# A hybrid decoder layer on one Trainium2 core: the scheduler ranks instructions by the build's timeline model

## The chip, the cores and the metric

The kernel runs on one core of one Trainium2 chip. A core has five engines that run side by side, each through its own queue of instructions in a fixed order: TensorE (PE, matrix products; its weight loads are shown apart as PEld), VectorE (DVE), ScalarE (ACT), GpSimd (POOL) and SyncE (SP). Engines wait for one another by semaphores. An instruction that waits holds up everything behind it in its own queue. DMA transfers are started by instructions of SP, ACT or POOL and then run by themselves.

The metric is the device time of one execution in microseconds (us). The kernel before took 2222.85, 2223.15 and 2224.5 us in three runs; the median is 2223.15 us.

## The reference

One layer of a decoder on 512 tokens of width 2048, in float32, with one batch:

```python
mod = silu(c) @ W_ada + b_ada                # shift1, scale1, gate1, shift2, scale2, gate2
h   = rms_norm(x, norm1_g) * (1 + scale1) + shift1
u   = h @ w_in                               # columns: 3 x 1024 conv, 1024 q, 6 x 256 k/v, 24 gates
y_conv = u_b * causal_conv3(u_c * u_h)       # 1024 channels
y_attn = g0 * compressed + g1 * selected + g2 * sliding_window      # 8 heads of 128, 2 k/v heads
x   = x + gate1 * (concat(rms_norm(y_conv), rms_norm(y_attn)) @ w_out)
h   = rms_norm(x, norm2_g) * (1 + scale2) + shift2
x   = x + gate2 * (relu(h @ w_ff1) ** 2 @ w_ff2)                    # hidden width 8192
return rms_norm(x, normf_g)
```

With 512 tokens there are 8 blocks of 64 tokens and up to 16 may be selected, so the selected branch sees every earlier token, and so does the sliding window of 512. The compressed branch attends to 31 blocks made by a small two-layer network (`compress`).

## The kernel before

**Layout.** Activations lie transposed: 128 channels on the partitions, 512 tokens along the free axis. Weights come as blobs of 128 x 1024 float32 (512 KB).

**Every product is three matmuls.** A float32 operand is split into a high part, rounded to the narrower type that PE takes at full rate, and a low part, the rest. `split`, `weights` (L76) and `hilo` (L799) do this: the high part is a copy on ACT (L83, L89, L800), the low part a subtraction on DVE (L84, L90, L801). `mm3` then issues L93 (high x high), L94 and L95 (the two mixed products). So a weight blob goes through DMA, ACT and DVE before PE can use it: L93 and L94 need only ACT's part of the blob, L95 needs DVE's part; L94 takes the low part of the activations.

**Buffers.** Raw blobs of the first half lie in three `raw` buffers (L72), loaded through SP's queue (L73) and free again when L84 has read them. In the feed-forward part there are six buffers `rw` (L791) for raw blobs, three pairs `hl` (L796) for split ones, two `sg` for sums of blobs and three `gt` for results on their way out.

**Stages, with the stretch of the profiled execution that each takes (us).**

- 0–184: the first projections (`w_kv`, `w_cv`) with the first norm and parts of the modulation vectors `mod`. Its instructions go through `pin` (L67), which calls `tc.keep_in_program_order` while `pinned[0]` is true (set at L98, cleared at L411). Their order is the written one.
- 184–584: the remaining projections (`project`, L429), with `compress` (L446) for the compressed branch, and in turn with them `ada` (L142, its loads at L147, its sums at L134), which works out the rest of `mod` on DVE, one vector of weights after another.
- 584–778: attention (`attention`, L654) over 2 groups of heads and 4 blocks of queries. Scores go to PSUM tiles `s` (three banks, L673–L676), their maxima and exponentials to DVE and ACT; the score's first 32 columns are moved by DVE to `pc` (L683); then come transposes (L719), splits of the transposed probabilities `tt`, and the products with the values in the one bank `pv`. Behind each block follow its squares (L733), their sum over heads (L737) and over channels (L739). Between the blocks `out_conv` (L641) issues the output projection of the conv half: 16 calls with 24 matmuls each into a tile `pw`, and L650 adds the residual.
- 778–794: the norm of the attention half. `tot` (L760) sums the squares; `row_bcast` (L175, L761) takes the root on ACT (L178) behind a table load, makes a diagonal on DVE, spreads it by PE (L197) and copies it on ACT (L182) into `rc`. A loop over eight tiles scales `ya` (L766) and splits it into `mixa` (L769), with the last two calls of `out_conv` at j = 0 and j = 4.
- 794–880: the output projection of the attention half, first 1024 columns (`w_oa`), with the last eight vectors of `mod`; the other 1024 columns (`late_out`) use blobs kept split in spare buffers.
- 880–960: preparation of the feed-forward tokens. `low_tokens` (L888) and `high_tokens` (L897) scale by the second norm and make seven combinations of tokens (B1, U6, T5, B2, T7, B3, T4), each split in high and low. The first products run in between (`ahead`, L962).
- 960–1540: first feed-forward product (`ff1`, L971), 32 steps. Each step loads four blobs, and `operands` (L918) makes seven weight operands of them (sums at L875, splits at L800 and L801); seven products of half size take the place of eight (a Strassen-like scheme). Results are squared, combined, split into `gt` and written to DRAM tensors `g` through POOL's queue (L1015, L1019).
- 1540–1600: the handoff. Token tiles `tk` of the second product are read back from `g` through the same queue (L1121), and the residual from `x1d` (L1086).
- 1600–2140: second feed-forward product, 8 x 4 steps of the same scheme.
- 2140–2222: the last quarter step in plain products (`plain`, L1091) and the final norm (`finish`, L1056).

**What sets the order.** The kernel is written in Tile: the program's text states operations on tiles; a scheduler takes the instructions that the text issues, ranks them by a model of how long each takes, and writes for each engine a queue in the order that the ranking gives. Buffers go to tiles, and waits to instructions, by that order. Only instructions that are kept in program order (the pinned stage) stay as written. So a matmul of `out_conv` needn't stand where the text has it.

## Time and profile before

The rows that the prediction shows aren't repeated here. The span is the time from the first to the last instruction on the core; the profiled execution's own time lies around it.

| what | value |
|---|---|
| median of three runs | 2223.15 us |
| lowest and highest | 2222.85 and 2224.5 us |
| the profiled execution's own time | 2224.19 us |
| its span | 2222.4 us |
| mean granted clock of PE | 0.981 |
| DMA, read and written | 383.00 and 68.16 MB, 203 GB/s |

The busy shares of PE, DVE and the DMA engines in 40 equal slices of the span (55.6 us each, in tenths) and the granted clock:

```profile
PE   6999989999999999799999999999899999999997
DVE  8889978877496687999999999999799999999996
PEclk7999999999999999899999999999999999999998
DMA  8985686954211165276665666658865466366442
```

PE is at least 90% busy in 35 slices of the 40. The lower ones are the first, those that begin at 278, 889 and 1556 us, and the last: the first loads, the projections, the token preparation, the handoff between the two feed-forward products, and the final norm.

How to read the rows below: in a timeline a row has the start, the duration, the engine, the line of the kernel, the operation, output<-inputs with their shapes, and in brackets the idle time of the engine before it with what ended it. In a table of waits a row has the engine, its waiting tile and line, what it waited for, then total us, times and the longest. In a table of groups the numbers are the busy time and the mean ns of one, then the idle time just before the group's instructions. Durations of matmuls overlap, since they are pipelined.

### The profile page before, as it was taken

Reading aid. Unit: us, or ns where it says so; the run is one execution under the profiler, and the core shown is the slowest. Engines: PE = TensorE matmul, PEld = TensorE weight load, DVE = VectorE, ACT = ScalarE, POOL = GpSimd, SP = SyncE. Lnnn points to the kernel's source line nnn. Section 1 sums busy time; section 2 is a strip of 40 time slices with the busy share of each in tenths; the row PEclk is TensorE's granted clock in tenths of the full one; section 3 lists DMA queues with packets and bytes.
Section 4 is the critical chain, followed back from the end, with each engine's and each line's share of the span. In section 5 each row is a group of like instructions: output and inputs, shape, how many; then the busy total and the mean of one; then the engine's idle time right before and its main releaser. Section 6 shows DMA issues by size and latency. Waiting matters only on the chain.

```text
span 2222.4 us, 37637 instructions
## 1 busy us (share of the span) xinstructions
PE 2131.6 (96%) x14942; PEld 1969.9 (89%) x14942; DVE 1918.1 (86%) x2998; ACT 1008.2 (45%) x1468; POOL 193.6 (9%) x366
## 2 busy tenths in 40 slices
PE   6999989999999999799999999999899999999997
PEld 4777778898777779799999999999899999999996
DVE  8889978877496687999999999999799999999996
ACT  4431333222354435665666556666333333333353
POOL 0000000000000001021111111113211011011000
PEclk7999999999999999899999999999999999999998
DMA  8985686954211165276665666658865466366442
GB/s 343 336 323 180 237 313 256 356 216 180 86 39 57 57 266 185 81 233 209 199 196 195 199 211 196 201 190 283 296 241 195 157 237 233 119 237 235 151 146 95
DMA packets 143984, 453.61 MB, mean 204 GB/s; under 512 B 15809, under 2 KB 20161, under 8 KB 143809
## 3 DMA queue, kind: packets, MB, share of 16 engines
q1 hardware_dynamic: 91104, 322.22, 40.4%
q0 software_dynamic: 51616, 127.95, 17.2%
q8 instruction: 117, 1.92, 0.3%
q10 hardware_dynamic: 1088, 1.05, 0.1%
q14 instruction: 59, 0.48, 0.1%
HBM read 383.00 MB, written 68.16 MB: 203 GB/s over the span
## 4 chain that ended last, share of the span: by engine, by line
PE 75%; DVE 13%; ACT 5%; DMA 4%; issue 2%; SPq 0%; DVEq 0%; ACTq 0%; POOL 0%; POOLq 0%
PE pf L95 18%; PE pf L93 18%; PE pf L94 18%; PE ps L94 5%; PE ps L95 5%; PE ps L93 5%; DVE scr L134 3%; DVE wl L84 2%; DMA tk<-g 1%; DVE hl L801 1%; ACT wh L83 1%; PE pw L94 1%; PE pw L95 1%; PE pw L93 1%; PE pt L719 1%
## 5 line engine op out<-in xcount | busy, mean ns | idle before, releaser
L93 PE MATMUL pf<-tk,hl 128*128 128x256 f32 x3576 | 1008.0, 282 | 12.3 <-DMA tk<-g 6.0
L95 PE MATMUL pf<-tk,hl 128*128 128x256 f32 x3576 | 1005.5, 282 | 12.2 <-DVE hl L801 12.2
L94 PE MATMUL pf<-tk,hl 128*128 128x256 f32 x3576 | 1006.7, 282 | 1.3 <-DVE tk L872 1.3
L93 PEld LDWEIGHTS pf<-tk,hl 128*128 128x128 f32 x3576 | 678.2, 190 | 15.3 <-ACT hl L800 8.0
L95 PEld LDWEIGHTS pf<-tk,hl 128*128 128x128 f32 x3576 | 676.7, 190 | 14.8 <-DVE hl L801 14.7
L94 PEld LDWEIGHTS pf<-tk,hl 128*128 128x128 f32 x3576 | 677.0, 189 | 1.7 <-DVE tk L872 1.6
L800 ACT ACTIVATE hl<-rw 128x1024 fp32r<-128x1024 f32 x264 | 278.8, 1056 | 303.6 <-PE pf L95 254.9
L801 DVE TENSOR_TENSOR hl<-rw,hl 128x1024 fp32r<-128x1024 f32 x264 | 321.9, 1219 | 25.6 <-ACT hl L800 25.2
L800 ACT ACTIVATE hl<-sg 128x1024 fp32r<-128x1024 f32 x189 | 200.3, 1061 | 267.7 <-PE pf L95 242.9
L801 DVE TENSOR_TENSOR hl<-sg,hl 128x1024 fp32r<-128x1024 f32 x189 | 230.5, 1221 | 41.7 <-ACT hl L800 41.3
L134 DVE SCALAR_TENSOR_TENSOR scr<-wa,cs 128x1024 bf16<-128x1024 f32 x176 | 211.0, 1220 | 8.1 <-DMA wa<-in_w_ada 8.0
L83 ACT ACTIVATE wh<-raw 128x1024 fp32r<-128x1024 f32 (+1 forms) x105 | 110.8, 1059 | 221.0 <-PE ps L94 105.1
L84 DVE TENSOR_TENSOR wl<-raw,wh 128x1024 fp32r<-128x1024 f32 (+1 forms) x105 | 128.6, 1225 | 56.6 <-ACT wh L83 54.2
L875 DVE TENSOR_TENSOR sg<-sg,rw 128x1024 f32<-128x1024 f32 x126 | 153.5, 1219 | 0.9
L95 PE MATMUL ps<-h_m,wl 128*128 128x512 f32 x360 | 142.8, 397 | 2.5 <-DVE wl L84 2.4
L93 PE MATMUL ps<-h_m,wh 128*128 128x512 f32 x360 | 142.6, 396 | 2.4 <-ACT wh L83 1.2
L94 PE MATMUL ps<-h_m,wh 128*128 128x512 f32 x360 | 141.8, 394 | 0.0
L1049 DVE SCALAR_TENSOR_TENSOR x<-pf,mod,x 128x256 f32<-128x256 f32 x256 | 119.7, 479 | 17.9 <-PE pf L95 14.9
L93 PE MATMUL ps<-h,wh 128*128 128x512 f32 x280 | 113.2, 404 | 13.1 <-ACT wh L83 9.1
L95 PE MATMUL ps<-h,wl 128*128 128x512 f32 x280 | 113.7, 406 | 2.4 <-DVE wl L84 2.4
L94 PE MATMUL ps<-h,wh 128*128 128x512 f32 x280 | 113.3, 405 | 0.0
L1015 POOL DMA_DIRECT2D g<-gt x192 | 101.0, 532 | 86.4 <-DVE gt L872 81.2
(325 smaller groups left out, 2974.1 us busy)
## 6 DMA issues: line engine op xcount, KB each, us to landing
rw<-in_w_f SPq DMA_DIRECT2D x262, 512.0 KB, 4.3
wa<-in_w_ada SPq DMA_DIRECT2D x176, 512.0 KB, 6.2
tk<-g POOLq DMA_DIRECT2D x114, 512.0 KB, 8.1
g<-gt POOLq DMA_DIRECT2D x192, 256.0 KB, 5.0
raw<-in_w_conv SPq DMA_DIRECT2D x32, 512.0 KB, 6.6
raw<-in_w_kv SPq DMA_DIRECT2D x16, 512.0 KB, 5.4
raw<-in_w_cv SPq DMA_DIRECT2D x16, 512.0 KB, 4.5
raw<-in_cmp_w SPq DMA_DIRECT2D x16, 512.0 KB, 5.4
```

What stands on the lines that cost most here:

```text
L83: pin(nc.scalar.activation(wh[:, :cols], raw[:, :cols], AF.Copy))
L84: pin(nc.vector.tensor_tensor(out=wl[:, :cols], in0=raw[:, :cols], in1=wh[:, :cols].bitcast(F32), op=OP.subtract))
L93: pin(nc.tensor.matmul(ps, lh, rh, start=start, stop=False, skip_group_check=more))
L94: pin(nc.tensor.matmul(ps, lh, rl, start=False, stop=False, skip_group_check=more))
L95: pin(nc.tensor.matmul(ps, ll, rh, start=False, stop=stop, skip_group_check=more))
L134: pin(nc.vector.scalar_tensor_tensor(out=scr, in0=w, scalar=1.0, in1=cs[i].rearrange("p a b -> p (a b)"), op0=OP.mult, op1=OP.mult, accum_ ...
L719: nc.tensor.transpose(pt[:, r * P:(r + 1) * P], probs[b, r][:, kb * P:(kb + 1) * P], ident)
L800: nc.scalar.activation(dst[0], src, AF.Copy)
L801: nc.vector.tensor_tensor(out=dst[1], in0=src, in1=dst[0].bitcast(F32), op=OP.subtract)
L875: nc.vector.tensor_tensor(out=dst, in0=x, in1=y, op=op)
L1015: nc.gpsimd.dma_start(out=gd[p // 4][idx[j]][p % 4 // 2][:, p % 2], in_=g[:, j])
L1049: nc.vector.scalar_tensor_tensor(out=xm, in0=src, scalar=gate, in1=xm, op0=OP.mult, op1=OP.add)
```

## The change

One argument of the scheduler's context changes. Without it, instructions are ranked by the scheduler's default model of durations; with it, by a simulated timeline of the build. The text of the kernel, its tiles, pools and buffers stay, and so does `keep_in_program_order` for the first stage.

```diff
@@ -1246,7 +1246,7 @@
     args = {k[3:]: nc.dram_tensor(k, v.shape, mybir.dt.from_np(v.dtype), kind="ExternalInput").ap()
             for k, v in arrays.items()}
     out = nc.dram_tensor("out", OUT_SHAPE, F32, kind="ExternalOutput").ap()
-    with tile.TileContext(nc) as tc:
+    with tile.TileContext(nc, schedule_with_timeline_sim=True) as tc:
         hybrid_layer(tc, args, out)
     r = run_bass_kernel_spmd(nc, [arrays], core_ids=[0])
     return unpack(r.results[0]["out"])
```

What that does to the queues can be listed from the two builds, since each engine's instructions stand in a fixed order:

| engine | instructions | at another place | first difference |
|---|---|---|---|
| PE | 14898 | 5266 | 807th |
| DVE | 2807 | 1617 | 269th |
| ACT | 1409 | 619 | |
| POOL | 363 | 34 | 226th |
| SP | 623 | 78 | 126th |

Each engine's first difference lies behind the pinned stage. The places that the prediction goes through: loads of `raw` stand ahead of some of `ada`'s in SP's queue, and blocks of `compress` alternate with halves of a `project` block on PE; at the start of attention 24 `pw` matmuls stand ahead of the fourth score tile; all `out_conv` matmuls stand ahead of the last block of attention, none behind it; in DVE's queue eight L766 and two L650 stand ahead of the first low split of `mixa`; in the token preparation three L875 sums of weights and the low splits of weights stand ahead of token operations; in the steady steps of the feed-forward products two high products of the next operand stand in front of the 24 matmuls before them; at the handoff the token loads L1121 follow each other in POOL's queue, with the writes L1015 and L1019 behind them.

## Prediction

> **What bounds the kernel now.** I read the page's summary first, then the busy time by stretches (bounds set at the stages), then what TensorE (PE) waited for in each, and single instructions.
>
> ```profile
> span 2222.4 us, 37637 instructions
> PE 2131.6 (96%) x14942; PEld 1969.9 (89%) x14942; DVE 1918.1 (86%) x2998; ACT 1008.2 (45%) x1468; POOL 193.6 (9%) x366
> PE 75%; DVE 13%; ACT 5%; DMA 4%; issue 2%; SPq 0%; DVEq 0%; ACTq 0%; POOL 0%; POOLq 0%
> ```
>
> PE is busy in 96% of the span. No matmul is added or removed, so an order can win only what PE now idles (2222.4 − 2131.6 = 90.8 us) and the share in which its clock is low. Where that lies:
>
> ```profile
> core 0: us, PE busy (x) PEld busy (x) DVE busy (x) ACT busy (x) POOL busy (x), PEclk, DMA share, GB/s
> 0.00:184.00 184.00, 159.57 (x623) 120.21 (x624) 160.30 (x285) 71.76 (x94) 0.20 (x4) 0.94 0.84 313
> 184.00:584.00 400.00, 387.49 (x1937) 323.78 (x1936) 319.41 (x520) 125.44 (x160) 0.00 (x0) 0.99 0.65 243
> 594.00:607.00 13.00, 10.56 (x43) 9.26 (x43) 7.33 (x32) 5.18 (x20) 0.00 (x0) 0.61 0.24 83
> 607.00:778.00 171.00, 165.38 (x859) 130.69 (x858) 128.38 (x313) 82.50 (x216) 0.00 (x0) 1.00 0.14 50
> 778.00:794.00 16.00, 15.68 (x67) 11.84 (x66) 11.86 (x19) 9.41 (x17) 0.00 (x0) 1.00 0.29 99
> 880.00:960.00 80.00, 65.59 (x461) 62.64 (x460) 74.70 (x137) 52.52 (x102) 5.74 (x10) 0.87 0.32 109
> 960.00:1540.00 580.00, 579.50 (x4913) 578.75 (x4912) 534.89 (x715) 359.46 (x507) 112.76 (x215) 1.00 0.64 204
> 1540.00:1600.00 60.00, 51.60 (x414) 50.84 (x414) 46.77 (x63) 24.09 (x32) 18.14 (x34) 0.94 0.99 362
> 1600.00:2140.00 540.00, 540.00 (x4582) 540.00 (x4581) 498.71 (x692) 209.83 (x211) 51.07 (x95) 1.00 0.55 199
> 2140.00:2222.00 82.00, 64.89 (x519) 62.11 (x517) 64.70 (x116) 35.99 (x68) 0.00 (x0) 0.93 0.27 91
> ```
>
> Columns: length, busy time of each engine with its number of instructions, granted clock (1.00 is full), DMA share. The first 184 us hold 24.4 us of the idle time, but their written order stays: nothing to win or lose. The two feed-forward stretches (960–1540 and 1600–2140) idle 0.50 and 0.00 us in 1120: they can only lose. What is open lies between: projections 12.5, start of attention 2.4 and half a clock, attention 5.6, its tail 0.3, token preparation 14.4, the handoff from the first to the second feed-forward product 8.4, the end 17.1; the 5 us left over lie in 794–880, at the first w_oa weights, whose place doesn't change.
>
> **The change part by part.** Every engine keeps its number of instructions; their order changes. In the changed build 5,266 of PE's 14,898 instructions stand at another place, 1,617 of DVE's 2,807, 619 of ACT's 1,409, 34 of POOL's 363 and 78 of SP's 623, the first in each behind the pinned stage. I follow the new order through each stretch.
>
> *Projections and compression, 184–584.*
>
> ```profile
> PE ps L93 <- ACT wh L83: 7.4, 3, 6.1
> SPq L73 <- DVE wl L84: 25.0, 7, 7.4
> ```
>
> First row: PE's largest wait of the stretch (total, times, longest). Second: SP's queue between 240 and 300 us stood 25.0 us for the raw buffers (three, freed by the low split at L84), with weight loads of the modulation vectors (L147) in turn with the raw loads. The new order puts raw loads ahead of some L147 loads and interleaves a compression block with halves of a projection block, so PE has two streams to choose from. A raw load earlier in SP's queue still waits for the same buffer, and now holds the L147 loads behind it, for which DVE's L134 sums wait; those have slack until L650. I take half of the 7.4: −4, between −10 (that and two or three of the small waits) and +4 (the blocked L147 loads cost half of the longest wait, 7.4).
>
> *Start of attention, 594–607.*
>
> ```profile
> 594.28 0.44 PE L93 MATMUL pw<-mix,wh 128*128 128x512 f32 x1
> 597.16 0.50 PE L673 MATMUL s<-kslc,q 128*128 128x160 f32 x1 [2.44 <-DVE pc L683]
> ```
>
> PE stands 2.44 us because the fourth score tile needs a bank that DVE frees at L683. The new order has 24 matmuls of the filler (output projection of the conv half, tile pw) ahead of that fourth score. At 0.25 us each (14.23 us for 57, the tail's first row below) they last 6 us and cover the 2.44. The clock of 0.61 over 13 us costs up to 10.56 × 0.39 = 4.1 more if it follows from the gap. Gain 2.4 to 6.5; I take −5 with −2 and −7 as bounds.
>
> [...]
>
> *Attention, 607–778.*
>
> ```profile
> PE pt L739 <- DVE sr L737: 2.1, 7, 0.5
> PE pv L93 <- ACT tt L89: 1.6, 5, 0.6
> ```
>
> The filler is issued earlier and in larger groups, so more PE work stands between a score and its transposes (8.9 us before, 16.8 after, median, by counting matmuls of each order at their traced spacing). Only 5.6 us are idle; I take half, −3, bounds −5.6 and 0.
>
> *The tail, 778–794: the price.* All filler now stands ahead of the last block, so the norm of the attention half runs bare.
>
> ```profile
> 778.00:794.00 16.00, 14.23 (x57) 10.49 (x57) 1.49 (x2) 1.00 0.29 99
> 778.27 0.60 ACT L733 ACTIVATE sq<-pv 128x512 f32<-128x512 f32 x1 [1.55 <-PE pv L95]
> 780.12 0.35 PE L739 MATMUL pt<-ones,sr 128*128 128x1 f32 x2 [0.24 <-DVE sr L737]
> 780.85 1.06 ACT L83 ACTIVATE wh<-raw 128x1024 fp32r<-128x1024 f32 x1 [1.30 <-PE pw L94]
> 781.93 1.28 ACT L178 ACT_TABLE_LOAD   x1
> 784.60 1.10 PE L197 MATMUL pt<-dg,ones 128*128 128x512 f32 x2
> 785.74 0.60 ACT L182 ACTIVATE rc<-pt 128x512 f32<-128x512 f32 x1 [2.21 <-PE pt L197]
> 788.36 0.68 DVE L90 TENSOR_TENSOR mixa<-ya,mixa 128x512 fp32r<-128x512 f32 x1
> L766 DVE SCALAR_TENSOR_TENSOR ya<-ya,vec,rc 128x512 f32<-128x512 f32 x8 | 5.6, 746 | 1.9 <-ACT rc L182 1.9
> L650 DVE SCALAR_TENSOR_TENSOR x<-pw,mod,raw 128x512 f32<-128x512 f32 x16 | 11.9, 747 | 12.4 <-PE pw L95 12.3
> PE pf L95 <- DVE wl L84: 1.3, 1, 1.3
> ```
>
> First row: of the 16 us, 57 filler matmuls are 14.23; in the changed order there are none. What is left is the chain: square (778.27), sum over partitions, root, the diagonal broadcast (L197), rc, the scaled ya (L766), the split of mixa, the first matmul of w_oa. The root now begins at 783.2, behind a weight split (780.85) and the table load (781.93). That split is gone from ACT's queue here: the table load follows the copies of the square's block and is over when the sum arrives (780.12 + 0.35 and two small DVE steps, about 780.9). So everything from the root on comes 2.3 us earlier: rc at 785.74 − 2.3 = 783.4, done at 784.0. In DVE's new order eight L766 and two L650 stand ahead of the first low split. They follow each other at about 0.66 (the 746 ns of a record overlap): 784.0 + 10 × 0.66 + 0.68 = 791.3. Until then PE can do L197 (1.1), the sum (0.2) and eight high products of the first block (1.9). Idle: 791.3 − 778.3 − 3.2 = 9.8. To that 2 at half a clock (as behind the gap at 594) and 1.5, since the last block has lost its filler as well; minus 1.3, the weight split's wait of the last row, which falls away. Sum +12; bounds +8 (clock stays, last block covered) and +15 (the table load isn't earlier).
>
> *Token preparation, 880–960.* DVE is busy 74.70 of 80: it is the bound.
>
> ```profile
> PE pf L95 <- DVE hl L801: 9.2, 6, 3.1
> 897.46 1.23 DVE L875 TENSOR_TENSOR sg<-rw 128x1024 f32<-128x1024 f32 x1 [1.05 <-DMA rw<-in_w_f]
> ```
>
> The new order puts the low splits of weights (L801) ahead of the token operations, and moves three such L875 sums of 1.22 us out of the stretch into DVE's idle time before 895. At most 3 × 1.22 plus half the 9.2 leave, 8; with rises in the clock (0.87) 12. Against it: the sum at 897.46 waited for a load, and one put ahead of the tokens blocks DVE until it lands. −4, bounds −12 and +4.
>
> *Feed-forward steps.* In steady steps two high products of the next operand stand 24 matmuls (2.8 us) earlier.
>
> ```profile
> 1209.52 1.06 ACT L800 ACTIVATE hl<-rw 128x1024 fp32r<-128x1024 f32 x1 [1.47 <-PE pf L95]
> ```
>
> This high half is there at 1210.58; its first product ran at 1215.0 and would now run at 1212.2, with 1.6 us to spare. The low halves' products stay. Moved DVE work is covered by PE's queue as long as DVE, at 92% (534.89 of 580), doesn't fall behind: 0. If that cover goes, about 1 us a step (one L875 of 1.22 in front of a low split).
>
> *Handoff, 1540–1600.*
>
> ```profile
> PE pf L93 <- DMA tk<-g: 6.0, 2, 5.4
> 1553.69 0.54 POOL L1019 DMA_DIRECT2D g<-gb  x1 [4.85 <-DVE gb L90]
> 1554.22 0.54 POOL L1121 DMA_DIRECT2D tk<-g  x1
> ```
>
> POOL's queue stands 4.85 us at a write that waits for DVE, with token loads behind it, and PE waits 6.0 for those. The new order has the token loads whose data are already written ahead of these writes. But the DMA share is 0.99: earlier issues also collide with the weights. −5, bounds −10 (both waits and the clock) and +2 (later writes, later last tokens).
>
> *The end, 2140–2222.*
>
> ```profile
> PE pf L93 <- ACT hl L800: 3.4, 3, 1.3
> 2195.00:2222.00 27.00, 14.02 (x109) 12.96 (x107) 15.18 (x30) 5.62 (x14) 0.00 (x0) 0.79 0.45 155
> ```
>
> Of the 17.1 us idle 13.0 lie in the last 27, mostly the final norm's chain, which no order shortens. Sums (L875) move up, so their buffers and the loads behind them come earlier. Most of the 3.4: −3, bounds −4 and +1.
>
> **Sum.** −4 −5 −3 +12 −4 +0 −5 −3 = −12. The profiled execution took 2224.19 us (span 2222.4 and 1.8 around it), so 2212.2; it lay 1.04 above the median of the runs (2223.15), so the forecast is 2211 us. Its own range, from the bounds as independent errors (about 6, 2, 3, 3.5, 8, 6, 2.5: root of the squares 13), is 2198 to 2224.
>
> **The rivals.** *The bare tail decides (slower).* The chain at 778–791 takes its full price of 12 to 15, and the places that should repay it don't: their waits end on buffers and loads that keep their times. For it: the tail's price is the only one worked out from an uninterrupted chain, each other gain rests on a queue that may wait elsewhere. Against: the 2.44 and 4.85 us stalls have their work visibly moved in between. 2223.15 + 13 = 2236. It decides once the gains elsewhere are under 12.
>
> *Gains cancel the tail.* They come to 8 to 16: within 4 us of before, 2223. The gains I list are 24, so this needs half of them to fail.
>
> *All places pay and the tail is partly hidden.* Near the favourable bounds: −8 −6 −5 +8 −8 −7 −3 = −29, 2194. For it: 14.4 + 12.5 + 8.4 us are idle there. Against: 880–960 is bound by DVE's work, which stays.
>
> *DVE late in the feed-forward.* A sum moved in front of a low split delays it in every step of one half: 29 steps (without the three prepared ahead) by 1 us is 2252. For: DVE's 92%. Against: 0.50 us idle in 580 now, and the splits I followed keep over 1.5 us.
>
> That the change does nothing is excluded: the orders differ.
>
> **How the numbers follow.** Forecast 0.46, bare tail 0.23, cancelling 0.13, all pay 0.13, DVE late 0.05. Within 0.2% (4.4 us, about what a measurement of this kernel can tell from no change): 0.13 + 0.02 of the forecast's edge. Faster: 0.43 + 0.13 = 0.56. Slower: 0.23 + 0.05 + 0.01 = 0.29. Range 2192 to 2240: it holds the bare tail up to +17 and most of the last gain, and leaves out some 0.15.
>
> **What would show it.** Tail: no pw matmul behind the last PV product, and a PE idle time of 8 to 12 us released by DVE mixa. Start of attention: no L673 waiting for pc there, clock over 0.9. Handoff: the wait for tk under 3 us. 880–960: PE's waits for L801 under 5 us. Feed-forward: idle still under 3 us in 960–1540 and 1600–2140. Wrong if the tail's gap is hidden, if the four repaying places keep their waits, or if the feed-forward stretches lengthen.

## The result, and the profile after

The changed kernel took 2234.95, 2235.9, 2237.0 and 2240.42 us, median 2236.45; the kernel before, beside it, 2223.59. The ratio is 1.0059, 95% interval 1.0047 to 1.0071: 13 us slower. The profiled execution took 2234.95 us with a span of 2233.0.

From the page of the changed kernel, the span, the busy times and the chain that ended last by engine:

```profile
span 2233.0 us, 37645 instructions
PE 2129.7 (95%) x14942; PEld 1974.4 (88%) x14942; DVE 1915.9 (86%) x2998; ACT 1012.9 (45%) x1468; POOL 194.4 (9%) x366
...
PE 80%; DVE 14%; ACT 3%; issue 2%; DMA 1%; SPq 0%; DVEq 0%; ACTq 0%
```

The busy times are those of before. The changed kernel, by the stretches of before (the last is 10 us longer):

```profile
core 0: us, PE busy (x) PEld busy (x) DVE busy (x) ACT busy (x) POOL busy (x), PEclk, DMA share, GB/s
...
184.00:584.00 400.00, 391.19 (x1965) 327.54 (x1965) 318.53 (x520) 126.96 (x161) 0.00 (x0) 1.00 0.66 245
594.00:607.00 13.00, 12.22 (x74) 9.97 (x72) 9.76 (x40) 7.22 (x23) 0.00 (x0) 1.00 0.22 81
607.00:778.00 171.00, 154.12 (x762) 126.98 (x762) 117.68 (x284) 74.45 (x195) 0.00 (x0) 0.93 0.14 50
778.00:794.00 16.00, 14.94 (x80) 11.28 (x78) 9.41 (x19) 6.38 (x11) 0.00 (x0) 1.00 0.18 67
794.00:810.00 16.00, 5.31 (x13) 2.62 (x12) 10.92 (x19) 8.28 (x16) 0.00 (x0) 0.67 0.04 7
880.00:960.00 80.00, 61.92 (x408) 57.04 (x407) 67.67 (x129) 48.71 (x100) 3.30 (x5) 0.79 0.24 82
960.00:1540.00 580.00, 575.62 (x4886) 575.10 (x4885) 528.50 (x706) 359.73 (x502) 108.86 (x206) 1.00 0.65 201
1540.00:1600.00 60.00, 60.00 (x511) 60.00 (x510) 56.23 (x80) 34.02 (x48) 22.74 (x43) 1.00 1.03 358
1600.00:2140.00 540.00, 540.00 (x4573) 540.00 (x4572) 500.28 (x685) 203.35 (x195) 54.86 (x102) 1.00 0.58 208
```

Read against the same rows of before: the start of attention (594–607) is almost whole, 12.22 of 13 busy at full clock. But in 607–778 PE now idles 16.9 us (5.6 before) and the clock is 0.93. The tail's gap is in 794–810, where PE works 5.31 of 16. The handoff (1540–1600) has no idle time left.

Since stretches of equal time no longer hold equal work, I also compared the traces at points where both have issued exactly the same set of matmuls. At such a point the time since the first matmul can be subtracted. The differences, changed minus before, for the stages between such points (named by the time of before), and the same for the runs below:

```
us against the profiled execution of before; the first column holds the pinned stage too
                                    -482  -793  -814  -878  -978 -1540 -1593 -2144 -2211   sum
changed kernel                      -7.9  14.3   7.3  -1.4  10.0  -0.5 -11.4   1.3  -0.8  10.9
c1 before, its order written out     1.2  -1.5   1.8   0.0   0.3   0.0  -0.4   0.0   0.1   1.5
e1 attention and tail back          -3.6  -2.6   1.6  -1.3  11.1   2.3 -10.2   2.1   0.5  -0.1
e2 token preparation back           -3.7  13.8   7.3  -1.5   3.8   1.3 -11.3   1.7  -0.6  10.8
e3 both back                        -4.8  -1.1   0.4  -1.4   4.4   1.9 -11.4   2.1  -0.7 -10.5
e4 before, projections changed      -7.5  -2.6   2.3   0.2  -0.2   1.9   0.5   2.2   0.0  -3.2
e5 before, POOL's queue changed     -1.3  -1.5   1.6   0.0   0.9   0.0   3.1   0.0   0.0   2.8
e6 filler spread                    -4.7  14.7   6.8  -1.5   9.5   1.4 -11.3   1.7  -0.1  16.2
e7 sums early                       -4.1  14.5   6.9  -1.5   9.6   1.4 -11.4   1.7  -0.1  16.9
e8 bank early                       -8.8  14.2   4.0  -1.5  10.0   1.4 -11.3   1.7  -0.1   9.5
e9 filler for the tail              -4.0  18.5  -1.3  -1.3  10.1   0.8 -11.2   1.4   0.6  13.5
e10 first attention blocks back     -5.3   3.4   7.7  -1.4  10.2   1.0  -9.9   1.9  -0.7   6.8
e11 before, handoff changed          0.0  -1.5   1.3   0.0   1.1   0.0  -9.3   0.0   0.1  -8.4
e12 norm's sum first                -7.1  14.1   7.3  -1.5  10.0   1.4 -11.4   1.7  -0.1  14.5
e13 changed, no late rotations      -6.7   7.3   7.3  -1.6  10.1   1.4 -10.4   2.8   0.6  10.6
e14 before, no late rotations       -0.5  -2.1   1.9   0.0   0.7  -0.6   0.1  -0.6   0.1  -1.1
e15 before, projections and handoff -4.6  -1.1   3.2   0.2  -1.1   1.9 -11.4   3.1  -0.1  -9.9
```

The second row is the program of before in another execution: it shows how far such a column moves by itself, up to 1.8 us. The first column moves more: where the projections have the changed order it lies anywhere from −3.6 to −8.8. In the columns to 793 and 814 the profiled execution of before is itself off by some 1.5 us, one up and one down: c1, e5 and e11, with the order of before there, have −1.5 and 1.3 to 1.8. In the first row the two places that should repay (−7.9 and −11.4) paid more than was forecast, and two places where a gain was forecast, attention and the token preparation, lost 14.3 and 10.0.

What PE waited for there, in the changed kernel (first four rows 600–710 us, the next three 780–815, the last two 880–975):

```profile
PE pt L739 <- DVE sr L737: 5.2, 3, 2.5
PE pv L94 <- DVE tt L90: 3.1, 6, 1.1
PE s L673 <- ACT q L284: 2.7, 1, 2.7
PE pt L719 <- DVE ssq L740: 2.4, 2, 2.0
...
PE pf L93 <- ACT mixa L89: 6.9, 1, 6.9
PE pt L739 <- DVE sr L737: 1.8, 1, 1.8
PE pt L197 <- DVE dg L188: 1.8, 1, 1.8
...
PE pf L94 <- DVE tk L872: 6.8, 6, 2.5
PE pf L93 <- ACT tk L871: 6.0, 4, 2.7
```

None of these is among the large waits of before. The old waits are gone or small, as forecast (pc at L683, token loads from `g`); the new ones are all for work of DVE or ACT.

### The profile page after: what moved, and what is told of

It is laid out like the page before. It is cut to its first block, busy times and chain, and to the rows that moved or that the text cites. A ratio compares the mean times of both kernels' runs of the same rounds, so it can differ in the third digit from the quotient of the medians.

```text
span 2233.0 us, 37645 instructions
## 1 busy us (share of the span) xinstructions
PE 2129.7 (95%) x14942; PEld 1974.4 (88%) x14942; DVE 1915.9 (86%) x2998; ACT 1012.9 (45%) x1468; POOL 194.4 (9%) x366
## 4 chain that ended last, share of the span: by engine, by line
PE 80%; DVE 14%; ACT 3%; issue 2%; DMA 1%; SPq 0%; DVEq 0%; ACTq 0%
PE pf L93 19%; PE pf L95 19%; PE pf L94 19%; PE ps L95 5%; PE ps L94 5%; PE ps L93 5%; DVE scr L134 3%; DVE wl L84 2%; PE pw L93 1%; PE pw L95 1%; PE pw L94 1%; DVE hl L801 1%; PE pt L719 1%; ACT wh L83 1%; DVE x L1049 1%
## 5 line engine op out<-in xcount | busy, mean ns | idle before, releaser
L93 PE MATMUL pf<-tk,hl 128*128 128x256 f32 x3576 | 1000.5, 282 | 16.3 <-ACT tk L871 6.0
L94 PE MATMUL pf<-tk,hl 128*128 128x256 f32 x3576 | 1000.9, 282 | 8.0 <-DVE tk L872 6.8
L95 PE MATMUL pf<-tk,hl 128*128 128x256 f32 x3576 | 981.7, 282 | 2.0 <-DVE hl L801 2.0
L800 ACT ACTIVATE hl<-rw 128x1024 fp32r<-128x1024 f32 x264 | 279.6, 1060 | 292.2 <-PE pf L95 215.7
L801 DVE TENSOR_TENSOR hl<-rw,hl 128x1024 fp32r<-128x1024 f32 x264 | 322.0, 1220 | 36.1 <-ACT hl L800 35.7
L800 ACT ACTIVATE hl<-sg 128x1024 fp32r<-128x1024 f32 x189 | 200.5, 1061 | 288.3 <-PE pf L95 283.1
L801 DVE TENSOR_TENSOR hl<-sg,hl 128x1024 fp32r<-128x1024 f32 x189 | 230.4, 1220 | 35.8 <-ACT hl L800 35.8
L83 ACT ACTIVATE wh<-raw 128x1024 fp32r<-128x1024 f32 (+1 forms) x105 | 110.9, 1060 | 235.4 <-PE ps L94 131.3
L875 DVE TENSOR_TENSOR sg<-sg,rw 128x1024 f32<-128x1024 f32 x126 | 153.4, 1217 | 0.0
L1049 DVE SCALAR_TENSOR_TENSOR x<-pf,mod,x 128x256 f32<-128x256 f32 x256 | 118.9, 479 | 16.3 <-PE pf L95 12.3
L1015 POOL DMA_DIRECT2D g<-gt x192 | 101.4, 533 | 252.7 <-DVE gt L872 238.3
```

What stands on the lines that cost most here:

```text
L83: pin(nc.scalar.activation(wh[:, :cols], raw[:, :cols], AF.Copy))
L93: pin(nc.tensor.matmul(ps, lh, rh, start=start, stop=False, skip_group_check=more))
L94: pin(nc.tensor.matmul(ps, lh, rl, start=False, stop=False, skip_group_check=more))
L95: pin(nc.tensor.matmul(ps, ll, rh, start=False, stop=stop, skip_group_check=more))
L800: nc.scalar.activation(dst[0], src, AF.Copy)
L801: nc.vector.tensor_tensor(out=dst[1], in0=src, in1=dst[0].bitcast(F32), op=OP.subtract)
```

## The experiments

All sixteen kernels hold an order by edges between neighbours of a queue, which order issue and add no wait. The order is written out as a list of instruction numbers for each engine; with the list of before's order it is the program of before (run c1), and the scheduler's option is then not needed.

```diff
+    have = {i.name: i for i in nc.cur_bb.bb.instructions}
+    for steps in json.loads(zlib.decompress(base64.b85decode(ORDER))).values():
...
+            last, name = name, f"I-{at}"
+            if last is not None:
+                tc.add_manual_dep(have[name], last, mybir.DependencyInfo(
+                    mybir.DependencyClass.NoSync, mybir.DependencyReason.DATA), reason="order")
```

Below, an edit is shown as what changes in these lists. "Before" and "changed" name the order taken for the instructions that the kernel before starts in the given time.

### Stage by stage

```diff
 e1:  changed
+e1:  482-800 before
 e2:  changed
+e2:  880-980 before
 e3:  changed
+e3:  482-800 before, 880-980 before
 e4:  before
+e4:  up to 482 changed
```

> Every queue has the changed kernel's order, except that the instructions which the kernel before starts between 482 and 800 us (attention, its tail) have the order of before. Theory (the loss is made stage by stage, each by its own order, and the stages add): counted at points where both traces have issued the same matmuls, the changed kernel loses 21.5 us between 482 and 814, so 2236.5 - 21.5 = 2215. Rival (the lost time is shared: attention's delay lets DVE and the loads of the next stages run ahead, so they give it back): less than half returns, 2226 or more. The start of attention again shows PE waiting about 2.4 us for pc, and the granted clock there falls to about 0.6.

Measured: 2221.28 us beside 2223.56 (0.9992, 0.9982 to 1.0002), 15 us under the changed kernel. In the table, the two columns to 814 go from 21.6 to −1.0. The loss in attention and its tail is that stage's own order. The expected 2215 wasn't reached: in the trace the first column gives 4.3 us less than in the changed kernel, and the two feed-forward columns take 3.6 more. At the start of attention PE waits for `pc` again (2.4 us in two), and the clock over 594–604 is 0.83.

> The changed kernel's order, with the order of before only for the instructions that the kernel before starts between 880 and 980 us (token preparation). Theory: the 10 us lost there come back, 2226.5, and PE's waits for token tiles (12.8 us) give way to the old waits for split weights (9.2). Rival: the stage is bound by DVE's work in any order and the loss is only moved there from the first feed-forward steps, so the time stays within 3 us of 2236.

Measured: 2234.62 (1.0046, 1.0034 to 1.0058); the stage goes from 10.0 to 3.8. Between the two: 6 us of 10 return in the trace, and the time, 1.8 under the changed kernel, hardly shows them. Part of the difference is in the first column, −3.7 here and −7.9 in the changed kernel's execution: the rest of what is missing there lies in the feed-forward columns (3.0 against 0.8). PE's old waits are back, as expected, and one of them is longer than before, for the sum of squares of the second norm (1.7 us before):

```profile
PE pf L95 <- DVE hl L801: 9.1, 5, 3.1
PE pf L171 <- DVE sacc L810: 5.0, 1, 5.0
```

> Both stages (482-800 and 880-980) in the order of before, all else in the changed order. Theory: 2236.5 - 21.5 - 10 = 2205, faster than either kernel, since the projections' gain (7 to 8) and the handoff's (11) are kept. Rival: the gains at the handoff and in the projections exist only because of the changed stages between them, and the time is that of before, 2223.

Measured: 2213.5 (0.9952, 0.9940 to 0.9964), 10 us faster than before. The gains in the projections and at the handoff don't depend on the stages between them. The time is 8.5 us above the expectation. In the trace 4.4 are left in the token stage, the first column gives 3.1 less than in the changed kernel, and the two feed-forward columns take 3.2 more.

> The order of before, with the changed order only for the instructions that start before 482 us (in effect 184-482, projections and compression). Theory: the gain of that stage stands alone, 2223.6 - 7 = 2216.5, with PE's 6.1 us wait for ACT's split at L83 gone. Rival: the gain is taken back at the start of attention, because its inputs (q, the filler's weights) come no earlier: 2221 to 2224.

Measured: 2223.06 (1.0000, 0.9990 to 1.0011). The trace won 7.5 us by 482, kept them to 978, and lost 4.1 in the two feed-forward stretches, whose order is that of before. The same two windows, 1000–1500 us, of c1 and of e4:

```profile
1000.00:1500.00 500.00, 500.00 (x4246) 500.00 (x4245) 458.64 (x611) 308.69 (x435) 93.72 (x178) 1.00 0.63 199
```

```profile
1000.00:1500.00 500.00, 500.00 (x4232) 500.00 (x4231) 456.94 (x605) 305.74 (x428) 92.66 (x176) 1.00 0.65 200
```

PE has no idle time and full clock in both, and does 14 matmuls less: 118.1 ns each against 117.8 (500 us by the counts). Neither named theory said that. The written lists of c1 and e4 are the same behind PE's 2051st instruction, so the order of that part isn't the cause. c1, e5 and e11, with the projections of before, agree with before to 0.0 us in those columns. Since buffers go to tiles by the order, the tiles of the feed-forward part may lie elsewhere in e4; whether they do, and whether that costs the 4 us, no run shows.

```diff
 c1:  (scheduler's order)
+c1:  before, written out
```

> The order of before, written out in full as a list, as in the other runs here. It is the same program as before, so 2223 to 2224 within 0.2%. It shows what of the profile of before was chance: the projections alone (e4) won 7.5 us in the profile by 482 us but only 0.5 in the runs. Theory: PE's 6.1 us wait for L83 at 280 us is a load that landed late in that one execution, and is absent or smaller here. Rival: it is there again, and the projections' gain was lost elsewhere.

Measured: 2223.81 beside 2224.82 (0.9996, 0.9986 to 1.0005). The rival holds: the 6 us wait is there again (7.5 us in three for L83, 7.4 before; in c1 the trace stays within 1.4 us of before at every point to 482). So the projections' gain is real: the thirteen traces with the changed projections have −3.6 to −8.8 in the first column, the four with those of before −1.3 to 1.2. Of e4's 7.5 us, 4.1 were lost in the feed-forward columns.

### The handoff

```diff
 e5:  before
+e5:  POOL's queue changed (34 places)
 e11: before
+e11: 1500-1605 changed, all engines
```

> The order of before on PE, DVE, ACT and SP; only POOL's queue has the changed order (34 of 362 places, at the handoff between the feed-forward products). Theory (token loads stood behind writes that waited for DVE): PE's 6.0 us wait for the token loads goes, with the clock loss behind it; 2223.6 - 8 to 11 = 2212.6 to 2215.6. Rival (it needs PE's and DVE's new order too, or the transfers are limited by the DMA engines, share 0.99): within 3 us of 2223.6.

Measured: 2227.3 (1.0011, 1.0003 to 1.0020): slower. The wait for token loads went, and another came. In e5, PE's largest wait in 1540–1610 and what ACT did ahead of it:

```profile
PE pf L93 <- ACT hl L800: 9.3, 1, 9.3
```

```profile
1560.29 0.63 ACT L871 ACTIVATE gt<-gx 128x512 fp32r<-128x512 f32 x1 [5.83 <-DMA g<-gt]
1560.83 1.04 ACT L800 ACTIVATE hl<-rw 128x1024 fp32r<-128x1024 f32 x1
```

The writes of `gt` now stand behind the token loads, so the three `gt` buffers come free later; ACT's L871 stands 5.83 us for one, and L800, which splits the weights that PE needs, stands behind L871.

> The order of before, with the changed order of all engines for what starts between 1500 and 1605 us (the handoff). With POOL's queue alone PE's wait for token loads turned into one of 9.3 us for ACT's L800, which stood behind L871, which waited for the writes of gt. Theory (the gain needs ACT's and DVE's new order beside POOL's, and nothing of earlier stages): no such wait, 9 to 11 us gained in the stage, 2213 to 2215. Rival (it needs the earlier stages' order, or is luck of one execution): under 3 us.

Measured: 2214.14 (0.9958, 0.9941 to 0.9974), 9.4 us faster than before, the stage −9.3. The row of e11 that answers to the handoff's before:

```profile
1540.00:1600.00 60.00, 58.68 (x494) 58.06 (x493) 54.02 (x75) 28.27 (x37) 17.68 (x33) 1.00 1.04 380
```

The DMA share of 1.04 (380 GB/s) is no lower than before (0.99, 362 GB/s), with PE busy 58.68 us against 51.60, so the transfers were not the limit; the queues were.

### Attention

> The changed order with one edit in attention: the pw matmuls of output-projection blocks 4 to 7 and the end of block 3, which stand in three lumps there, are spread over 605 to 708 us, each block within what its banks and weight buffers allow (the splits of the later blocks move behind). Theory (attention loses because PE has nothing but attention's own chain between the lumps): of the 10 us lost between 482 and the tail, 6 to 10 return: 2227 to 2231, and the granted clock between 610 and 710 is 0.95 or more (0.51 to 0.92 in five windows before). Rival (DVE's order is to blame, the filler only fills): under 3 us, since the waits for L737, L740 and L284 stay.

```diff
 PE, 599-708 us of the changed kernel
-blocks 4, 5 in 617-635; blocks 6, 7 in 667-683
+blocks 4, 5 over 617-662; blocks 6, 7 over 667-708; the end of block 3 over 605-615
```

Measured: 2236.64 (1.0061, 1.0048 to 1.0073), the stage 14.7 against 14.3. Nothing returned, and the clock stayed low (0.89 over 586–710, 0.90 in the changed kernel).

> The changed order with one edit in attention: on DVE the sums over heads (L737) and the copies of their totals (L740) stand right where their inputs are there, ahead of the rotations of q, splits and residuals that the changed order puts before them (up to 2.1 and 3.9 us earlier); PE's order stays. Theory (filler in lumps): PE's next waits take over, under 3 us gained, 2234 to 2236. Rival (DVE's order): the waits for L737 (5.2 us in attention) and L740 (2.4) go, and with them half-clock stretches: 5 to 8 us, 2228 to 2231.

```diff
 DVE, at 641-644 us of the changed kernel, and likewise behind the other blocks
-L272, L274, L276, L286, L740, L689
+L740, L272, L274, L276, L286, L689
```

Measured: 2241.07 (1.0083, 1.0070 to 1.0097), the stage 14.5. The rival falls too: the wait for L737 fell from 5.2 to 2.5 us, and the one for the low split `tt` rose from 3.1 to 6.1. In e7, 482–780:

```profile
PE pv L94 <- DVE tt L90: 6.1, 6, 4.2
```

So neither edit by itself returns anything. What both edits leave alone is how much DVE has to do before PE can go on. From the changed kernel, DVE at one such place, and the windows 604–614 and 684–694 with, below them, the filler's matmuls in the same windows:

```profile
641.38 0.68 DVE L272 TENSOR_TENSOR rt<-qr,rot 128x512 f32<-128x512 f32 x1
642.08 0.69 DVE L274 TENSOR_TENSOR rt<-qr,rot 64x512 f32<-64x512 f32 x1
642.78 0.69 DVE L276 TENSOR_TENSOR rt<-qr,rot 64x512 f32<-64x512 f32 x1
643.49 0.69 DVE L286 SCALAR_TENSOR_TENSOR q<-rs,q 128x512 fp32r<-128x512 f32 x1
644.10 0.15 DVE L740 COPY ssq<-pt 128x1 f32<-128x1 f32 x1
```

```profile
604.00:614.00 10.00, 7.02 (x43) 5.60 (x42) 9.40 (x30) 5.19 (x18) 0.00 (x0) 1.00 0.00 1
...
684.00:694.00 10.00, 7.48 (x36) 5.02 (x36) 6.75 (x9) 5.42 (x12) 0.00 (x0) 0.98 0.16 52
...
604.00:614.00 10.00, 0.00 (x0) 0.00 (x0) 0.00 (x0) 1.00 0.00 1
...
684.00:694.00 10.00, 0.00 (x0) 0.00 (x0) 0.00 (x0) 0.98 0.16 52
```

In 604–614 DVE works 9.40 of 10 us, and none of what PE does is filler. The rotations of the next q (L272 to L276) stand in DVE's queue in front of the copy L740, for which PE's transposes wait. In 684–694, again without filler, neither engine is full (7.48 and 6.75), so the amount of DVE's work isn't all of it.

```diff
 e10: changed
+e10: 482-700 before
 e13: changed
+e13: without L272, L274, L276, L278 of the last four heads
 e14: before
+e14: without L272, L274, L276, L278 of the last four heads
```

> The changed order, with the order of before only for what the kernel before starts between 482 and 700 us (attention's first blocks); the last blocks and the tail keep the changed order. Theory (attention's loss of about 10 us lies in those blocks, in the order of DVE, ACT and PE taken together; moving the filler or the sums alone won nothing): PE idles under 7 us in 586-710 (17 before) with a clock of 0.95 or more, the stage up to 793 gains 8 to 11, the tail's wait of 6 to 7 us stays; 2226 to 2229. Rival (the loss lies in the transition to the last blocks, which have most of the filler): it reappears there, under 4 us.

Measured: 2230.71 (1.0031, 1.0018 to 1.0045); the stage from 14.3 to 3.4; the tail's column stays (7.7 against 7.3). The windows 586–710 of the changed kernel, of e10 and of e13:

```profile
586.00:710.00 124.00, 107.05 (x542) 87.45 (x540) 86.89 (x239) 55.81 (x158) 0.00 (x0) 0.90 0.13 43
```

```profile
586.00:710.00 124.00, 115.19 (x594) 92.56 (x593) 93.81 (x256) 59.35 (x167) 0.00 (x0) 0.96 0.16 51
```

```profile
586.00:710.00 124.00, 110.27 (x573) 90.47 (x572) 81.93 (x237) 57.36 (x165) 0.00 (x0) 0.94 0.15 49
```

PE's idle time there falls from 17.0 to 8.8 us, with DVE busier (93.81 against 86.89): in the order of before the two work side by side, in the changed one more by turns. The time is 5.7 us under the changed kernel.

> The changed order, without the rotations of the last four query heads (16 DVE instructions, L272 to L278, about 11 us of DVE's work between 605 and 670 us; q is taken unrotated, so the output differs). Theory (in the stretches without filler DVE's queue is what PE waits for, and these rotations stand in it): the stage 482-793 gains 5 to 10. Rival (latency between the engines, not DVE's amount of work, sets those stretches): under 3. To be read against the same cut in the order of before.

> The order of before without the same 16 rotations (output differs). Theory: in that order filler covers DVE, PE idles 5.6 us in 607-778: under 2 us gained. Rival: 5 or more, as in the changed order; then the cut tells nothing of the order.

Measured: the stage to 793 gains 7.0 in the changed order (14.3 to 7.3) and 0.6 in that of before (−1.5 in c1 to −2.1). Both kernels leave the rotations out, so their output differs. In the stage, the same 11 us of DVE's work cost 7.0 us in the one order and next to nothing in the other. The times don't show this: e14 is 0.9989 (0.9980 to 0.9998), 2.9 us under before, and e13 1.0056 (1.0043 to 1.0070), 0.7 us under the changed kernel; in e13's trace the later columns and the first take back what the stage gained. Without the rotations q is also ready sooner, and PE's wait for it falls from 2.7 to 1.9 us, so the pair doesn't separate how much DVE has to do from how long the chain to q is.

### The tail

> The changed order with one edit on DVE in the tail: behind the second L766 come the first low split of mixa (L90) and the two L650 that free the filler's last banks, and then the other six L766 (in the changed order all eight L766 stand first, from 801.7 to 807.1 us, then L650). Theory (PE's 6.9 us wait, shown as one for ACT's split of mixa, is one for the bank that L650 frees at 807.8, since ACT's split was there at 803.2): PE starts w_oa some 3 to 5 us earlier, in the stage and in the time: 2231 to 2233. Rival (the wait is for ACT, as shown, or the later low splits take its place): the stage gains under 1 us.

```diff
 DVE
-L766 x8, L650 x2, L90 x8
+L766 x2, L90, L650 x2, L766 x6, L90 x7
```

Measured: 2240.18 (1.0071, 1.0054 to 1.0089) with runs from 2233.74 to 2242.48, so the time says nothing here; the stage 793–814 goes from 7.3 to 4.0. The tail's DVE queue in the changed kernel, and PE's wait in e8:

```profile
801.74 5.39 DVE L766 SCALAR_TENSOR_TENSOR ya<-ya,vec,rc 128x512 f32<-128x512 f32 x8 [2.65 <-ACT rc L182]
807.04 1.40 DVE L650 SCALAR_TENSOR_TENSOR x<-pw,mod,raw 128x512 f32<-128x512 f32 x2
```

```profile
PE pf L93 <- DVE x L650: 3.6, 1, 3.6
```

The wait of 6.9 us, shown as one for ACT, ended when the first L650 freed a bank; with L650 earlier it is 3.6 and has its right name. In e8 PE starts at 804.01 us, when six of ACT's eight splits of `mixa` are still to come.

> The changed order with the matmuls of the last two filler blocks (48) moved behind the last product with the values, around L739 and L197, and the splits of the first two w_oa blobs behind them. Theory (the bare tail costs 9 to 11 us since nothing covers the norm's chain): the 48 matmuls (about 11.5 us) cover the waits for L737, L188 and mixa (10.5 us): the stage up to the first w_oa products gains 7 to 10, time 2227 to 2229. Rival (the filler was covering waits where it stood, which come back there): under 3 us.

```diff
 PE
-pw 14, pw 15, last block, L739, L197, w_oa
+last block, 8 pw, L739, 14 pw, L197, 26 pw, w_oa
```

Measured: 2236.58 (1.0062, 1.0039 to 1.0084). Each half holds in its stage: 793–814 goes from 7.3 to −1.3, as the theory has it, and 482–793 from 14.3 to 18.5, where the 48 matmuls are now missing, as the rival has it. Of 8.6 us won, 4.2 come back; the time (runs from 2231.22 to 2243.47) doesn't show the rest, and the theory's 2227 to 2229 wasn't reached.

### Token preparation, and the two gains together

> The changed order with one edit on PE in the token preparation: the two L171 (sums of squares for the second norm, shown as x4) stand directly in front of 18 matmuls of the first feed-forward block that the changed order puts ahead of them. Their input was there at 911.4 us, they ran at 915.2, and ACT (6.6 us) and DVE (4.9 us) stood waiting behind them. Theory (DVE binds this stage, so what DVE idles there passes straight into the time): DVE's wait falls to about 1 us, the stage 878-961 gains 3 to 5, time 2231.5 to 2233.5. Rival (the stage loses by the weight sums and splits put among the token operations): under 1 us, since PE then waits as long for the later token splits.

```diff
 PE
-L95 (911.0), 18 matmuls of block 1, L171 x2
+L95 (911.0), L171 x2, 18 matmuls of block 1
```

Measured: 2241.76 (1.0085, 1.0070 to 1.0101), the stage 10.0, as without the edit. In the changed kernel DVE stands for the sum:

```profile
916.18 0.17 DVE L179 RECIPROCAL rs<-rs 128x2 f32<-128x2 f32 x1 [4.92 <-ACT rs L178]
```

and in e12, DVE's waits in 890–990, and below them ACT's largest in 890–930:

```profile
DVE hl L801 <- ACT hl L800: 5.7, 4, 4.3
...
DVE rs L179 <- ACT rs L178: 1.4, 1, 1.4
```

```profile
ACT hl L800 <- PE pf L95: 3.8, 1, 3.8
```

The wait for the root fell from 4.9 to 1.4, and one of 4.3 for a weight split took its place: ACT's L800 in turn waits 3.8 us until PE has read a buffer. The theory falls and the wait only changes its name.

> The order of before with the changed order in the two stages where it won: before 482 us and from 1500 to 1605. Theory (stages add): 2223.6 - 7.5 - 9.4 = 2206.7, less a gain if tiles of the feed-forward part come to lie elsewhere: with the projections changed alone, the 9500 matmuls of that part went from 117.8 to 118.2 ns each, 4 us, so 2207 to 2211. Rival (the projections' gain is worth nothing in most executions): 2214, as with the handoff alone.

```diff
 e15: before
+e15: up to 482 changed; 1500-1605 changed
```

Measured: 2214.06 (0.9960, 0.9948 to 0.9973), the time of e11. That is the rival's number, but not for its reason: the projections' gain is there (−4.6) and is paid back in the two feed-forward columns (1.9 and 3.1), as in e4.

## Why the prediction was wrong, point by point

- **Projections, −4.** Right: −7.9 in the trace of the changed kernel, of which 1.2 lie ahead of the changed part; −3.6 to −8.8 over the runs with that order. In e4 and e15 some 4 to 5 us of it went again in the feed-forward columns; in the changed kernel itself these columns are −0.5 and 1.3.
- **Start of attention, −5.** Right: the 2.44 us stall is gone and the clock is 1.00 in 594–607. In the kernel before it was 1.00 over 584–594 and 0.50 over 598–604, behind the gap; in e1, with 2.4 us of waits for `pc`, 0.83 over 594–604. In these three the clock went with the gap, as taken. The table doesn't separate this gain from the rest of its column.
- **Attention, −3, "bounds −5.6 and 0".** Wrong, and the step that failed most: 14.3 us lost to 793, some 3.6 of them the tail's two first waits (1.8 each, for L737 and L188). The step counted how much PE work stands between a score and its transposes and took that for cover. What PE waits for there is mostly DVE (5.2 us for L737, 3.1 for the split `tt`, 2.4 for L740), and the step never followed DVE's queue. In the changed order stretches with filler, in which DVE has time to spare, alternate with stretches without, in which DVE's chain holds PE up. e10, with the first blocks back in the order of before, returned 10.9 us of the stage and 5.7 of the time; e13 and e14 showed in the stage that DVE's rotations are on the path there and not in the order of before. The bound of 0 should have been open on the side of a loss.
- **The tail, +12.** Right in size: 7.3 in its column and the 3.6 just named, together 10.9. The way was half right: PE could not start with the high products, since banks came free only at L650, which stands behind the eight L766 (e8).
- **Token preparation, −4.** Wrong: +10.0. The prediction put three L875 sums of weights "into DVE's idle time before 895". In the changed kernel they run at 895.2, 899.0 and 900.5 us (some 883 to 888 on the scale of before), but in the middle of the token operations: DVE has no idle time there. The step counted the waits that leave and not those that come: PE's 9.2 us for L801 became 2.0, and 12.8 us for token tiles came instead. That the order is to blame is shown for 6 of the 10 us (e2), and of the 3.8 left there the longer wait for `sacc` accounts for 3.3 by its size. The late sum of squares is not the cause in the changed kernel (e12); which instructions are stays open.
- **Handoff, −5.** Right in direction, and larger than its bound of −10: −11.4. No wait for token loads, no clock loss. POOL's queue alone would have lost 3.1 (e5): the gain needs the other engines' new order as well, ACT's above all, and the prediction gave the credit to POOL.
- **Feed-forward steps, 0; the end, −3.** The steps were right: −0.5 and 1.3, and the 4.38 us idle in 960–1540 all lie ahead of 1000, in the token stage. The end was mis-sized: −0.8. The waits of 3.4 us for L800 went, and one of 4.3 for `x` (L1049) came.

The forecast was faster and the kernel is slower, with a time (2236) that the rival of the bare tail gave. Its place and price were right; its other half, that the repaying places don't pay, was not: projections and handoff paid 6.7 and 11.4 us, and attention and tokens took them back. That its time fits is luck. In both wrong terms the waits that the new order removes were priced, and those that it makes were not: in attention, DVE's queue was not followed at all; in the token stage DVE was named as the bound, but what its new order makes late for PE was not looked for.

On the clock: the attention step counted no loss of it. In the changed kernel the clock is 0.90 over 586–710 and 0.51 over 694–704, where PE is busy 8.90 of 10 us; the longest wait of PE in 586–710 is one of 2.7 us, for `q` (L284).

## What to carry to other kernels

A new order from a scheduler is many small changes, and its sum says little: here five stages moved by 7 us or more, two of them for the better. Take it apart by stages, keep the ones that win (the handoff alone: 2214.14 against 2223.52, faster than both kernels), and pin the rest. Measure the mix as well, since two stages that win need not add (e15). When work that fills one engine's gaps is moved, follow the queue of the engine that feeds it: cover counted on the waiting engine says nothing if the delivering one has other work in front.

## What the runs showed of the hardware

- The same feed-forward order ran at 117.8 ns a matmul in c1 and at 118.1 in e4, whose order differs only in the projections, at full clock and without a gap: 4 us in 9,500 matmuls. The cause is open.
- The granted clock was 0.61 over 594–607 in the kernel before, behind a wait of PE of 2.44 us, and 0.90 over 586–710 in the changed one, where PE's longest wait was 2.7 us.
- The engine that a table of waits names can be the wrong one. The 6.9 us shown for ACT's split in the changed kernel were a wait for a PSUM bank that DVE freed: with L650 earlier the wait was 3.6 us and shown for L650 (e8).
- In the kernel before, products of split parts with 512 columns started 0.23 us apart at full clock (589.73 to 592.75 us). The plain float32 product of that size at 784.60 us (L197) shows as two records, 1.10 us together.
